# Two numbers that order the gathers and the heads of a PEER layer: OWN 64 to 0, HEADS regrouped

## The chip, the core and the metric

The kernel runs on one core of a Trainium2 chip. The metric is the device time of one execution in microseconds; lower is better. Each execution computes the whole model below, once. Engines are named as in the profile: PE is TensorE, DVE is VectorE, ACT is ScalarE, POOL is GpSimd, SP is SyncE (here it only starts DMAs).

## The reference

The input is 256 tokens of width 1024 in float32. Two blocks follow each other. The first has two layers, each a mixer (neighbourhood attention in layer 0, a short convolution in layer 1) and then a PEER feed-forward; the second block is attention, retention and projections. The change lies in PEER, which is computed twice, once per layer:

```python
q = (xc @ w_query).reshape(c, 8, 2, 128)              # 8 heads, 2 halves
sc = einsum('chpd,hpnd->chpn', q, keys)               # against 128 sub-keys each
sv, si = top_k(sc, 16)                                # 16 best of each half
cand = sv[:, :, 0, :, None] + sv[:, :, 1, None, :]    # 16 x 16 sums
best, pos = top_k(cand, 16); eidx = cidx at pos       # 16 experts per head of 16384
g = softmax(best)
a = einsum('cd,chkd->chk', xc, w_up[eidx])            # one dot product per chosen expert
out = einsum('chk,chkd->cd', gelu(a) * g, w_down[eidx])
```

Each token so has 8 x 16 = 128 chosen experts, called its numbers; w_up and w_down have 16384 rows of 1024 values per layer.

## The kernel before, in words

`peer(l)` treats the 256 tokens in three sets.

- Tokens 0 to 159 (`TU = 160`) are computed densely: all 16384 experts are run through PE in 128 blocks of 128 experts (`up(i)`, line 704), gelu is applied, and the result is multiplied by a mask that holds the gates of the chosen experts and zero elsewhere.
- Tokens 160 to 191 (the set `also`, 32 tokens) have their 128 dot products formed from gathered rows of w_up; the results enter the same mask, and from there the dense path.
- Tokens 192 to 255 (the set `own`, 64 tokens) have both the rows of w_up and the rows of w_down gathered, and never touch the dense path before the end.

One gather is an indirect DMA that POOL starts (line 592): 128 rows of 1024 float32 values, one row per partition. For `own`, 64 tokens by 2 halves of their numbers fill the partitions, so it needs 64 gathers for the dot products and 64 for the rows of w_down; `also` has 32 tokens by 4 quarters and needs 32 gathers. That makes 160 in each layer. Four buffers hold them (`GB`), and a gather is started at most three ahead of its use (`LOOK`). A use is one DVE instruction: a multiply with a sum for a dot product (line 606), a multiply-add into an accumulator for a row of w_down (line 616; line 614 for the first). After the last dot product of a set, ACT applies gelu (line 608), DVE multiplies by the gate (line 609), and for `also` transposes the result into `gT` (line 611).

PEER has these stages. In the stage of the heads, q and the scores are formed head by head in the order `HEADS`, and the top-k steps run behind them on DVE and POOL. After every second head `numbers(n)` (line 661) copies those expert numbers that are complete on all partitions of a set into its index tile. In the up stage, 128 blocks of w_up come from memory in 64 loads of 1 MB, and for each PE does eight matmuls per block; beside them, `build()` makes the mask, four tokens at a time (48 builds for 192 tokens: ACT lines 732 and 733, DVE line 736, PE line 738, then DVE line 744 or ACT line 746 into the piece `A`). In the down stage, 128 blocks of w_down come in 64 loads of 1 MB (line 846); each is split into two parts by ACT (line 219, `whi`) and DVE (line 220, `wlo`), and PE does ten matmuls of 512 columns per block (lines 819 to 829). Its left sides come from `A`, split by ACT and POOL (lines 756 and 757 for tokens 0 to 127, 842 and 843 for the rest).

The order of the work is set by the Python program, and a list scheduler then moves instructions where their inputs allow it. In the up stage one gathered row is used per 1/0.97 blocks (`USES`). In the down stage the uses that are left are spread evenly over the first 122 blocks, each placed behind the `wlo` of its block. The list of gathers and the places at which it matters are these:

```python
order = dots(own)[:OWN] + [x for s in also for x in dots(s)]    # 579
n_dots = len(order)
order += dots(own)[OWN:] + [(own, "down", m) for m in range(own.n)]
...
def build():
    t = built
    while t >= TU and head < n_dots:      # tokens 160 and up: first use up n_dots gathers
        use()
...
n0 = head                                 # at the end of the up stage
while head < len(order) and n0 + (len(order) - n0) * i // (NK - 6) >= head:   # block i, down stage
    use()
```

Of the kernel before, what the change touches and what calls it, by code (L numbers as in the profile page):

```python
# [36 lines left out]
GB = 4  # L37
UB = 3
LOOK = 3
HEADS = (0, 4, 1, 5, 2, 6, 3, 7)  # L40
STEPS = 8
SCB = 6
USES = 0.97
OWN = 64
BEND = 4
TDELAY = 9
EARLY = (0, 0, 4, 4, 4, 4, 6, 6)
# [38 lines left out]
class Kern:  # L86
# [434 lines left out]
    def peer(self, l):  # L521
        nc, tc, a, h = self.nc, self.tc, self.a, self.h
        with ExitStack() as ctx:
# [54 lines left out]
            dots = lambda s: [(s, "dot", m) for m in range(s.n)]  # L578
            order = dots(own)[:OWN] + [x for s in also for x in dots(s)]
            n_dots = len(order)  # L580
            order += dots(own)[OWN:] + [(own, "down", m) for m in range(own.n)]
            tiles, chosen = {}, []
# [70 lines left out]
            def numbers(n):  # L653

                done = HEADS[: n + 1]
                for s in sets:
# [8 lines left out]
            old = []  # L665
            for n, hh in enumerate(HEADS):
                marks.append(len(steps))
# [94 lines left out]
            for n in range(PH):  # L762
                heads(HEADS[n])
                if n > 0:
# [911 lines left out]
```

## Time and profile before

| | us |
|---|---|
| Median of 3 runs (2219.02 to 2224.34) | 2223.98 |
| The profiled execution, its own time | 2221.52 |
| Its span, from the first to the last instruction | 2219.8 |
| PE busy in the span | 2074.6 (93%) |
| DVE busy in the span | 1615.1 (73%) |

The span of 2219.8 us has 1.7 us around it that the trace doesn't show. In the 40 slices of the page one slice is 55.5 us. PE is at 9 (90% or more) in most of them. The up stage of layer 0 runs from about 290 to 530 us and its down stage from about 586 to 884 us; in layer 1 these are about 1160 to 1401 and 1454 to 1749 us. Between the up and the down stage of each layer the PE clock row has a dip, and so has PE's busy row.

### The profile page before, as it was taken

The page shows a single profiled execution, that of the slowest core. Times are in us where ns is not written, and L with a number is a line of the kernel's source. Part 1 is how long each engine was busy: PE and PEld are TensorE (multiplying, and loading weights), DVE is VectorE, ACT ScalarE, POOL GpSimd, SP SyncE. Part 2 cuts the span into 40 slices and gives each one's busy share as a digit, 9 for nine tenths or more (in the row PEclk, how much of TensorE's full clock was granted, in tenths as well). Part 3 has the DMA queues.
Part 4 walks back from the last instruction along what each step waited for, and adds up shares of the span by engine and source line. Part 5 has one row for each costly group of instructions (what it writes and reads, how often), then busy time and mean ns, then how long its engine had stood idle before and what let it go on. Part 6 is the DMA issues. An engine that isn't in the chain of part 4 may idle for free.

```text
span 2219.8 us, 34905 instructions
## 1 busy us (share of the span) xinstructions
PE 2074.6 (93%) x12576; PEld 1808.1 (81%) x12576; DVE 1615.1 (73%) x3458; ACT 1039.7 (47%) x2245; POOL 919.2 (41%) x780
## 2 busy tenths in 40 slices
PE   7999989995799999998898999499999999999998
PEld 6989989995677777998898999477777797568886
DVE  5869857786888887867865786778888766456674
ACT  4643225541555554544323553355555555445453
POOL 2437843334656663225863333575656111001100
PEclk9999999998799999999999999799999999699999
DMA  8576599999788886666579999888888664035543
GB/s 288 192 226 208 189 399 364 355 368 328 264 320 321 319 323 224 213 229 201 198 262 392 358 363 376 279 311 317 324 327 310 196 178 143 10 109 162 165 151 121
DMA packets 178733, 576.21 MB, mean 260 GB/s; under 512 B 16112, under 2 KB 77440, under 8 KB 145408
## 3 DMA queue, kind: packets, MB, share of 16 engines
q1 hardware_dynamic: 123840, 391.82, 50.6%
q0 software_dynamic: 48896, 172.25, 21.2%
q10 hardware_dynamic: 5824, 9.92, 1.5%
q8 instruction: 99, 1.62, 0.3%
q14 instruction: 74, 0.61, 0.1%
HBM read 568.49 MB, written 3.15 MB: 258 GB/s over the span
## 4 chain that ended last, share of the span: by engine, by line
PE 66%; issue 8%; DVE 7%; POOL 5%; DMA 3%; ACT 1%; POOLq 0%; DVEq 0%; ACTq 0%
PE acc L704 11%; PE acc L225 6%; PE acc L226 6%; PE acc L227 6%; PE acc L819 5%; PE acc L824 5%; PE acc L822 5%; PE acc L829 5%; PE acc L823 5%; POOL gt L592 3%; PE tp L738 3%; DMA gt<-in_peer_w_up_dram,one 2%; PE tp L1250 1%; DVE gt L606 1%; PE tp L1263 1%
## 5 line engine op out<-in xcount | busy, mean ns | idle before, releaser
L704 PE MATMUL acc<-one,up 128*128 128x160 f32 x4096 | 579.8, 301 | 13.7 <-DMA up<-in_up_T_dram 13.5
L704 PEld LDWEIGHTS acc<-one,up 128*128 128x128 f32 x4096 | 565.3, 192 | 15.1 <-issue 6.9
L220 DVE TENSOR_TENSOR wlo<-dn,whi 128x1024 fp32r<-128x1024 f32 x256 | 362.9, 1426 | 115.3 <-ACT whi L219 115.1
L219 ACT CAST whi<-dn 128x1024 fp32r<-128x1024 f32 x256 | 267.8, 1048 | 229.6 <-PE acc L824 178.1
L220 DVE TENSOR_TENSOR wlo<-raw,whi 128x1024 fp32r<-128x1024 f32 (+1 forms) x196 | 256.9, 1314 | 139.2 <-ACT whi L219 137.8
L592 POOL DMA_INDIRECT gt<-in_peer_w_up_dram,one x192 | 206.8, 1077 | 340.1 <-DVE gt L606 298.1
L606 DVE SCALAR_TENSOR_TENSOR gt<-gt,rows 128x1024 f32<-128x1024 f32 x192 | 239.5, 1258 | 100.4 <-DMA gt<-in_peer_w_up_dram,one 100.1
L219 ACT CAST whi<-raw 128x1024 fp32r<-128x1024 f32 (+1 forms) x212 | 219.9, 1038 | 197.9 <-PE acc L227 81.3
L592 POOL DMA_INDIRECT gt<-in_peer_w_down_dram,one x128 | 201.5, 1574 | 175.2 <-DVE rows L616 148.7
L819 PE MATMUL acc<-whi,ahl 128*128 128x512 f32 x512 | 201.9, 394 | 6.5 <-POOL ahl L843 6.5
L824 PE MATMUL acc<-whi,m 128*128 128x512 f32 x512 | 204.9, 400 | 2.2 <-POOL m L757 2.2
L829 PE MATMUL acc<-wlo,ahl 128*64 128x512 f32 x512 | 200.5, 392 | 0.0
L823 PE MATMUL acc<-wlo,o 128*128 128x512 f32 x512 | 200.2, 391 | 0.0
L738 PE MATMUL tp<-m,o 128*128 128x128 f32 x768 | 111.3, 297 | 67.4 <-DVE m L736 53.7
L616 DVE SCALAR_TENSOR_TENSOR rows<-gt,one,rows 128x1024 f32<-128x1024 f32 x126 | 163.6, 1298 | 7.1 <-DMA gt<-in_peer_w_down_dram,one 6.8
L822 PE MATMUL acc<-whi,o 128*128 128x512 f32 x512 | 163.5, 399 | 1.4 <-ACT o L756 1.4
L738 PEld LDWEIGHTS tp<-m,o 128*128 128x128 f32 x768 | 103.6, 210 | 72.1 <-DVE m L736 53.1
L715 ACT ACTIVATE one<-acc 128x320 f32<-128x320 f32 (+14 forms) x112 | 41.0, 367 | 226.9 <-PE acc L704 226.8
L819 PEld LDWEIGHTS acc<-whi,ahl 128*128 128x128 f32 x512 | 96.6, 189 | 58.9 <-POOL ahl L843 7.7
L225 PE MATMUL acc<-xhi,whi 128*128 128x256 f32 x448 | 129.0, 290 | 0.8 <-ACT xhi L170 0.8
L732 ACT ACTIVATE o<-one,one 128x128 f32<-128x128 f32 x384 | 122.7, 401 | 11.6 <-PE tp L738 11.3
L226 PE MATMUL acc<-xlo,whi 128*128 128x256 f32 x448 | 128.0, 287 | 0.0
(350 smaller groups left out, 4168.8 us busy)
## 6 DMA issues: line engine op xcount, KB each, us to landing
up<-in_up_T_dram SPq DMA_DIRECT2D x128, 1024.0 KB, 7.7
dn<-in_down_P_dram SPq DMA_DIRECT2D x128, 1024.0 KB, 6.4
raw<-in_l_w_in_dram SPq DMA_DIRECT2D x84, 512.0 KB, 3.7
raw<-in_peer_w_query_dram SPq DMA_DIRECT2D x32, 512.0 KB, 4.8
raw<-in_l_w_out_dram SPq DMA_DIRECT2D x28, 512.0 KB, 3.5
raw<-in_attn_w_qkv_dram SPq DMA_DIRECT2D x24, 512.0 KB, 5.1
raw<-in_conv_w_in_dram SPq DMA_DIRECT2D x24, 512.0 KB, 4.5
raw<-in_attn_w_o_dram SPq DMA_DIRECT2D x8, 512.0 KB, 3.8
```

Of the source, the lines that this page charges most:

```text
L219: self.last_hi = nc.scalar.copy(hi[:, :n], raw[:, :n])
L220: self.last_lo = (eng or nc.vector).tensor_tensor(lo[:, :n], raw[:, :n], hi[:, :n].bitcast(F32), op=OP.subtract)
L225: nc.tensor.matmul(out, lhi, rhi, start=start, stop=False)
L592: nc.gpsimd.indirect_dma_start(out=t, out_offset=None, in_=rows[kind], in_offset=bass.IndirectOffsetOnAxis(ap=s.idx[:, m : m + 1], axis=0) ...
L606: nc.vector.scalar_tensor_tensor(t, t, 1.0, s.x, op0=OP.mult, op1=OP.mult, accum_out=s.dot[:, m : m + 1])
L704: nc.tensor.matmul(ps[:, j * TU : (j + 1) * TU], raw[:, j, c], x32[:, c], start=c == 0, stop=c == 7)
L738: nc.tensor.matmul(ps[:, j * P : (j + 1) * P], o2[:, j], m1[:, j], start=True, stop=True)
L819: both = lambda: nc.tensor.matmul(acc[1][q], hl[:, k], whi, start=i == 0, stop=i == NK - 1)
L822: nc.tensor.matmul(acc[0][q], hi[:, k], whi, **st)
L823: nc.tensor.matmul(acc[0][q], hi[:, k], wlo, start=False, stop=False)
L824: nc.tensor.matmul(acc[0][q], lo[:, k], whi, start=False, stop=i == NK - 1)
L829: nc.tensor.matmul(acc[1][q][:HALF], hl[:, k, :HALF], wlo, start=False, stop=False)
```

## The change

Two constants are changed, and nothing else.

```diff
-HEADS = (0, 4, 1, 5, 2, 6, 3, 7)
+HEADS = (0, 4, 2, 6, 1, 5, 3, 7)
-OWN = 64
+OWN = 0
```

With `OWN = 64` the list was: 64 dot products of `own`, 32 of `also`, 64 rows of w_down; `n_dots` was 96. With `OWN = 0` it is: 32 of `also`, 64 of `own`, 64 rows of w_down; `n_dots` is 32. The new `HEADS` completes the first 16 numbers of `also` after four heads (its quarters hold heads 0 and 1, 2 and 3, 4 and 5, 6 and 7). For `own` (halves: heads 0 to 3 and 4 to 7) 16, 16, 48 and 64 numbers are complete after two, four, six and eight heads, where it was 16, 32, 48 and 64. `numbers` issues 14 small copies per layer in place of 16.

What this does to the order is seen in three places of layer 0. In the names below, `rows192` is the activations of `own` or its accumulator, `rows160` those of `also`, `us` is an up block after gelu, `m1` and `o2` are a build's masks (or later the split of `A`).

On DVE, before, the end of the up stage:

```order
L606 SCALAR_TENSOR_TENSOR gt_930_5208,one272_272_1448<-gt_930_5208,rows160_269_1445 128x1024
L719 TENSOR_TENSOR one642_642_3378<-one642_642_3378,us_925_5192 128x2x160
L606 SCALAR_TENSOR_TENSOR gt_931_5211,one272_272_1448<-gt_931_5211,rows160_269_1445 128x1024
L606 SCALAR_TENSOR_TENSOR gt_932_5214,one272_272_1448<-gt_932_5214,rows160_269_1445 128x1024
L719 TENSOR_TENSOR one642_642_3378<-one642_642_3378,us_964_5334 128x2x160
L606 SCALAR_TENSOR_TENSOR gt_933_5217,one272_272_1448<-gt_933_5217,rows160_269_1445 128x1024
L719 TENSOR_TENSOR one642_642_3378<-one642_642_3378,us_975_5402 128x2x160
...
L606 SCALAR_TENSOR_TENSOR gt_953_5277,one272_272_1448<-gt_953_5277,rows160_269_1445 128x1024
L614 TENSOR_SCALAR rows192_962_5322<-gt_954_5280,one268_268_1444 128x1024
L609 TENSOR_TENSOR one273_273_1449<-one273_273_1449,one271_271_1447 128x32
L611 STREAM_TRANSPOSE one262_262_1438<-one273_273_1449 128x32
L736 TENSOR_SCALAR m1_959_5293<-one4_4_80,one260_260_1436,one262_262_1438 128x128 x4
```

The same place on DVE in the changed kernel:

```order
L606 SCALAR_TENSOR_TENSOR gt_940_5277,one267_267_1443<-gt_940_5277,rows192_264_1440 128x1024
L736 TENSOR_SCALAR m1_951_5329<-one4_4_80,one260_260_1436,one262_262_1438 128x128 x4
L606 SCALAR_TENSOR_TENSOR gt_945_5311,one267_267_1443<-gt_945_5311,rows192_264_1440 128x1024
L736 TENSOR_SCALAR m1_956_5363<-one4_4_80,one260_260_1436,one262_262_1438 128x128 x4
L719 TENSOR_TENSOR one642_642_3376<-one642_642_3376,us_925_5191 128x2x160
...
L719 TENSOR_TENSOR one642_642_3376<-one642_642_3376,us_986_5551 128x2x160
L220 TENSOR_TENSOR wlo_995_5575<-dn_993_5572,whi_994_5574 128x1024
L606 SCALAR_TENSOR_TENSOR gt_980_5523,one267_267_1443<-gt_980_5523,rows192_264_1440 128x1024
L220 TENSOR_TENSOR wlo_998_5592<-dn_993_5572,whi_997_5591 128x1024
L220 TENSOR_TENSOR wlo_1001_5608<-dn_999_5605,whi_1000_5607 128x1024
```

Before, the dot products of `also`, then 609 and 611, stand ahead of the masks of the last eight builds (first `m1_959`). Now those masks stand among the up blocks, and the first `wlo` of the down stage comes right behind the last `us`.

On PE, before, at the change from the up to the down stage:

```order
L704 MATMUL acc_1005_5574<-one263_263_1439,up_1004_5572 128x160 x16
L704 MATMUL acc_1013_5622<-one263_263_1439,up_1012_5620 128x160 x16
L738 MATMUL tp_957_5291<-m1_959_5293,o2_958_5292 128x128 x4
...
L738 MATMUL tp_1007_5586<-m1_1009_5588,o2_1008_5587 128x128 x4
L822 MATMUL acc_1019_5660<-whi_1025_5669,o2_1015_5634 128x512
```

The same place on PE in the changed kernel:

```order
L738 MATMUL tp_968_5443<-m1_970_5445,o2_969_5444 128x128 x4
L704 MATMUL acc_958_5383<-one263_263_1439,up_957_5381 128x160 x16
L738 MATMUL tp_976_5491<-m1_978_5493,o2_977_5492 128x128 x4
L704 MATMUL acc_966_5431<-one263_263_1439,up_965_5429 128x160 x16
L704 MATMUL acc_974_5479<-one263_263_1439,up_973_5477 128x160 x16
L704 MATMUL acc_982_5527<-one263_263_1439,up_981_5525 128x160 x16
L822 MATMUL acc_988_5565<-whi_994_5574,o2_984_5539 128x512
```

Eight groups of line 738 (one per build) stood behind the last up block; now they stand before it, and the first down matmul follows the last up matmul.

On DVE in the down stage, before, around the 40th block:

```order
L220 TENSOR_TENSOR wlo_1172_6388<-dn_1170_6385,whi_1171_6387 128x1024
L616 SCALAR_TENSOR_TENSOR rows192_962_5322<-gt_1144_6259,one268_268_1444,rows192_962_5322 128x1024
L220 TENSOR_TENSOR wlo_1175_6405<-dn_1170_6385,whi_1174_6404 128x1024
L220 TENSOR_TENSOR wlo_1178_6421<-dn_1176_6418,whi_1177_6420 128x1024
L616 SCALAR_TENSOR_TENSOR rows192_962_5322<-gt_1152_6306,one268_268_1444,rows192_962_5322 128x1024
L220 TENSOR_TENSOR wlo_1181_6438<-dn_1176_6418,whi_1180_6437 128x1024
```

And in the changed kernel, around the same block:

```order
L616 SCALAR_TENSOR_TENSOR rows192_1092_6054<-gt_1128_6224,one268_268_1444,rows192_1092_6054 128x1024
L220 TENSOR_TENSOR wlo_1152_6326<-dn_1150_6323,whi_1151_6325 128x1024
L616 SCALAR_TENSOR_TENSOR rows192_1092_6054<-gt_1137_6264,one268_268_1444,rows192_1092_6054 128x1024
L220 TENSOR_TENSOR wlo_1155_6343<-dn_1150_6323,whi_1154_6342 128x1024
L220 TENSOR_TENSOR wlo_1158_6359<-dn_1156_6356,whi_1157_6358 128x1024
L616 SCALAR_TENSOR_TENSOR rows192_1092_6054<-gt_1140_6281,one268_268_1444,rows192_1092_6054 128x1024
```

The down stage holds more uses per block than before. The program reaches its end of the up stage with 110 gathers used before and 80 now (before, the loop in `build()` ran 30 uses in one go just before block 114; now it finds `also` done some 35 blocks earlier), so 50 and 80 are left for the down stage of each layer.

## Rows read from the trace of the kernel before

**Rows 1.** Windows by stage: us, busy of PE, PEld, DVE, ACT, POOL, PEclk, DMA share, GB/s.

```profile
290.00:330.00 40.00, 33.10 (x232) 32.50 (x233) 22.51 (x53) 13.81 (x43) 12.30 (x12) 0.91 1.02 412
...
340.00:490.00 150.00, 150.00 (x1156) 150.00 (x1156) 118.23 (x369) 85.72 (x301) 50.71 (x48) 1.00 0.97 361
...
490.00:529.60 39.60, 38.99 (x283) 38.26 (x282) 22.58 (x43) 5.04 (x14) 15.05 (x14) 1.00 0.93 359
529.60:586.00 56.40, 17.88 (x75) 14.93 (x74) 45.70 (x77) 21.43 (x71) 35.36 (x29) 0.63 0.81 266
586.00:592.40 6.40, 6.40 (x16) 4.54 (x17) 3.39 (x3) 1.24 (x2) 5.28 (x4) 0.54 0.45 140
600.00:860.00 260.00, 260.00 (x1129) 199.62 (x1128) 213.09 (x159) 141.70 (x169) 154.87 (x101) 1.00 0.87 318
...
1401.30:1453.60 52.30, 18.48 (x74) 15.26 (x74) 41.85 (x73) 21.36 (x71) 33.89 (x27) 0.61 0.80 265
1470.00:1720.00 250.00, 250.00 (x1086) 191.89 (x1085) 204.85 (x153) 136.62 (x165) 150.25 (x98) 1.00 0.88 321
```

**Rows 2.** PE in order of time, layer 0: start, us, instructions, idle before and releaser.

```profile
411.31 1.50 PE L738 MATMUL tp<-m,o 128*128 128x128 f32 x12
412.65 4.51 PE L704 MATMUL acc<-one,up 128*128 128x160 f32 x32
...
520.71 8.93 PE L704 MATMUL acc<-one,up 128*128 128x160 f32 x64 [0.17 <-DMA up<-in_up_T_dram]
555.85 2.07 PE L738 MATMUL tp<-m,o 128*128 128x128 f32 x8 [26.20 <-DVE m L736]
...
585.96 0.79 PE L819 MATMUL acc<-whi,ahl 128*128 128x512 f32 x1 [4.36 <-POOL ahl L843]
```

**Rows 3.** The same in layer 1.

```profile
1383.63 17.63 PE L704 MATMUL acc<-one,up 128*128 128x160 f32 x128 [1.06 <-DMA up<-in_up_T_dram]
...
1453.57 0.51 PE L819 MATMUL acc<-whi,ahl 128*128 128x512 f32 x1 [2.17 <-POOL ahl L843]
```

**Rows 4.** DVE in order of time, layer 0, behind the dot products.

```profile
555.20 0.21 DVE L611 STREAM_TRANSPOSE one<-one 128x32 f32<-128x32 f32 x1
555.45 1.11 DVE L736 TENSOR_SCALAR m<-one,one,one 128x128 f32<-128x128 f32 x4
```

**Rows 5.** ACT in order of time, layer 0, around the last up block.

```profile
529.68 0.44 ACT L718 ACTIVATE us<-acc 128x320 f32<-128x320 f32 x1 [3.91 <-PE acc L704]
530.05 2.94 ACT L219 CAST whi<-dn 128x1024 fp32r<-128x1024 f32 x3
...
578.56 0.74 ACT L842 CAST ahl<-one 128x256 fp32r<-128x256 f32 x2
```

**Rows 6.** Lines 220, 616 (DVE), 757, 843 (POOL), 600 to 860 us: ns min/median/max.

```profile
L220 DVE TENSOR_TENSOR wlo<-dn,whi x113: 1207/1226/2927, 599.5 to 858.8; 128x1024 fp32r<-128x1024 f32 x113
  ACT whi L219: 47.3, 67
...
L616 DVE SCALAR_TENSOR_TENSOR rows<-gt,one,rows x46: 1270/1275/1280, 603.0 to 857.6; 128x1024 f32<-128x1024 f32 x46
...
L757 POOL TENSOR_TENSOR m<-one,o x29: 1282/1310/2282, 597.9 to 855.3; 128x512 fp32r<-128x512 f32 x29
...
L843 POOL TENSOR_TENSOR ahl<-one,ahl x28: 743/756/1725, 606.2 to 854.6; 128x256 fp32r<-128x256 f32 x28
```

**Rows 7.** Line 220 alone, same stretch: us, busy of DVE and POOL, PEclk, DMA, GB/s.

```profile
600.00:860.00 260.00, 160.74 (x113) 0.00 (x0) 1.00 0.87 318
```

**Rows 8.** DMA issues of 600 to 860 us: KB each, median us to landing.

```profile
dn<-in_down_P_dram SPq DMA_DIRECT2D x56, 1024.0 KB, 6.0
gt<-in_peer_w_down_dram,one POOLq DMA_INDIRECT x44, 7.2
```

**Rows 9.** The same for 340 to 490 us.

```profile
up<-in_up_T_dram SPq DMA_DIRECT2D x28, 1024.0 KB, 7.7
```

**Rows 10.** Line 606, 0 to 1000 us: what ended DVE's idle time (us, times).

```profile
  DMA gt<-in_peer_w_up_dram,one: 48.4, 25
```

## The prediction

> **What bounds the kernel now.** I read the windows by stage first, then PE in order of time where they show a hole, then the engines around it. In the steady up stage PE is busy 150.00 of 150 us and in the down stage 260.00 of 260 [rows 1]. A saving of work on DVE, POOL or DMA is worth nothing there. Between the two stages it is otherwise: from 529.6 to 586.0 us PE is busy 17.88 of 56.40 us, in layer 1 18.48 of 52.30, at a granted clock of 0.63 and 0.61 [rows 1]. The last up matmul of layer 0 ends at 520.71 + 8.93 = 529.64; then PE waits 26.20 us for line 736 on DVE, and the regular run of the down stage begins at 585.96 [rows 2]. Layer 1: 1383.63 + 17.63 = 1401.26 and 1453.57 [rows 3]. The mask of line 736 starts at 555.45, right behind the transpose of `also` at 555.20 [rows 4]. That is the forced loop in `build()`: tokens 160 and up want `gT`, and the list puts the 32 dot products of `also` behind all 64 of `own`, so the program uses 30 gathers in one go at block 114, and eight builds queue behind them. By the windows DMA is at 0.81 and DVE at 45.70 of 56.40 us [rows 1], so this is a chain of single gathers, masks and copies with PE idle.
>
> **What the change removes: the hole.** I count what PE does in it at full clock.
> - Eight builds are 64 records of line 738. Twelve take 412.65 - 411.31 = 1.34 us [rows 2], so 0.112 each and 7.1 us for 64.
> - A down matmul takes 260.00 / 1129 = 0.230 us [rows 1].
> - Layer 0, from 529.64 until the clock is back at about 592.4: 62.8 us, with 7.1 us of builds and 75 + 16 - 64 = 27 other records, some of the up stage's end; I take 24, 5.5 us. Lost: 62.8 - 7.1 - 5.5 = 50.2.
> - Layer 1: 52.3 us, at full clock from 1453.57 on, with 7.1 and 74 - 64 = 10 records, 2.3: lost 42.9.
> - Together 93 us.
>
> With the new list `also` is done after 32 uses, some 35 blocks before its first build, so its chain (lines 608, 609, 611) hides under up blocks. The eight builds go between the last up blocks, where PE pays their 7.1 us, already counted as work. What is late next is the start of the down stage. The last up block frees the buffer that the first `whi` needs, so behind its matmul ACT does 718 (0.44), 842 (0.74 for two, so 0.37) and 219 (2.94 for three, so 0.98) [rows 5]: 1.8 us, then 1.2 for `wlo` [rows 6]; PE has four matmuls (0.9) meanwhile. The second `wlo` stands behind a use, another 0.5 to 1.5. I take 4 us a layer with a dip of the clock, 8 in all; the bounds are 2 (the bare 1.8) and 12 (as long as the 6.4 us at clock 0.54 [rows 1], twice).
>
> **What it moves: 30 uses per layer into the down stage.** 110 gathers were used before that stage and now 80, so its first 122 blocks take 80 uses in place of 50: 0.656 per block instead of 0.41. A block is ten matmuls, 2.30 us of PE. Three things have to fit under it.
> - DVE is busy 213.09 of 260 us [rows 1]; 260 / 2.30 = 113 blocks, 1.89 us per block. A use is 1.275 us [rows 6] and overlaps its neighbour by some 0.07, so 0.246 x 1.2 = 0.30 more: 2.19 of 2.30, 95% in place of 82%. It fits, with 0.11 us to spare.
> - Contention with POOL takes from that. `wlo` has a median of 1.226 us and a maximum of 2.93 [rows 6]; its 113 sum to 160.74 [rows 7], 22.2 us more than 113 times the median. That is 0.39 us for each of the 57 instructions of lines 757 and 843 in the stretch, whose shortest take 1.28 and 0.74 [rows 6]. They now often fall into DVE's idle time (47.3 us of waits for `whi` [rows 6]), which the uses fill up.
> - DMA: a block loads 0.524 MB and gathers 0.656 x 0.524, 0.868 MB in 2.30 us, 377 GB/s, up from 318. The up stage carried 361 with PE full, and 412 was moved where PE waited [rows 1]. A load landed in 6.0 us in the down stage and 7.7 in the up stage [rows 8, 9]. By the buffers the load of a pair has about 8 us between the `wlo` that frees it and the cast that wants it, so slack is small.
>
> The nearest ends: 0 if all three stay under PE, and on the other side DVE blocked fully for each POOL instruction. Two lines, 1.28 + 0.74 us per four blocks, are 0.51 per block, of which 0.20 is paid: 1.89 + 0.30 + 0.31 = 2.50, 0.18 to 0.20 per block, 46 to 51 us over 256 blocks. DMA held to the up stage's 361 GB/s would be 0.868 / 0.361 = 2.40, 26 us. I take 0.07 per block, 18 us: half of the new POOL overlap plus scatter eats the 0.11 that is free and a little more.
>
> The Trainium skill, page "SBUF — State Buffer", section "Who interferes with whom", has the rule that speaks against this change: a DVE instruction with two SBUF inputs and a GpSimd instruction that reads SBUF exclude each other, and whoever comes second blocks until the first is done. The `wlo` rows, with a maximum of a whole instruction above the median, agree. By that rule the full end (46) becomes the sum where DVE has no idle time left, which is the second rival below; with the measured 0.39 carried over unchanged it would be 0.
>
> **What costs nothing.** The new `HEADS` reorders loads of equal size. The first 16 numbers of `also` are complete after four heads, the rest after eight; the first uses come behind the softmax in either kernel, so the gathers wait for nothing new; two fewer copies of `numbers` save POOL time that PE doesn't wait for. I allow 3 us either way. Gelu and gate of `own` now fall into the down stage, once per layer, DVE waiting for ACT: 1 to 2 us if DVE is full, inside the 18.
>
> **Sum.** 2221.5 (the profiled execution) - 93 + 8 + 18 = 2154.5. The median of the runs stands 2.5 above that execution, so 2157.
>
> **Rivals.**
> - Everything fits under PE: down blocks stay at 2.30 us. For it: none of DVE, ACT, POOL, DMA reaches its limit by the sums; against it: two of them are within 5%. 2139.
> - DVE becomes the bound of the down stage through the POOL contention: 46 in place of 18, 2185. For it: 95% before any new contention; against it: part of the POOL work still finds DVE waiting.
> - Slower than before: DVE waits for gathers. A use stands in DVE's queue ahead of the next `wlo`, so a late gather holds back PE. It decides from a loss of 85 us, 0.33 per block, (0.33 + 0.11) / 0.656 = 0.7 us of wait at each use; at 1.0 us it is (0.66 - 0.11) x 256 = 140 us, 2279. For it: 25 waits of 48.4 us in all for the dot products of layer 0 [rows 10]; against it: those are in stretches where uses are run as fast as the gathers land. The new pace, 2.30 / 0.656 = 3.5 us per use, is slower than the up stage's (a block's 0.524 x 1.97 MB at 361 GB/s are 2.9 us, a use per 2.9), where PE was full, and a gather is started three uses ahead, 10.5 us against 7.2 to landing [rows 8].
> - The change doesn't do what it says, since something else makes PE wait between the stages as long: within a few us of 2224. The order of the instructions speaks against it: the first down matmul stands behind the last up matmul.
>
> **How the numbers follow.** The forecast (2146 to 2170) has 0.58, DVE bound 0.19, everything under PE 0.14, slower 0.05, no effect 0.04. The range 2133 to 2190 takes in the second and the third. A measurement of this kernel can tell about 0.3% (7 us) from no change. Faster 0.91, same 0.04, slower 0.05.
>
> **What will show it.** Between the last matmul of line 704 and the first of 822 PE waits 2 to 5 us, not 26, and no line 738 stands in between; the clock stays near 1.0. Line 611 ends long before the first build of tokens 160 and up. In the down stage DVE is 92 to 98% busy, DMA 0.95 to 1.0 at 365 to 377 GB/s, PE 96 to 99%; where PE waits it is for `wlo`. It is wrong if PE waits there for gathers through line 616 or 606, if the loads of line 846 land late so that ACT waits for DMA, or if a block takes over 2.5 us.

## The result and the profile after

The changed kernel takes 2143.28 us (median of 4 runs, 2140.8 to 2145.78) against 2223.25 before (median of 4); the ratio is 0.9644 (95% interval 0.9625 to 0.9663). The forecast was 2157, its range 2133 to 2190. The profiled execution has a span of 2139.7 us, 80.1 less than the one before.

First the windows by stage of the changed kernel (columns as in [rows 1]); the stretches answer to the up stage, its end, the start of the down stage, and the down stage.

```profile
340.00:490.00 150.00, 150.00 (x1156) 150.00 (x1155) 118.94 (x372) 85.01 (x297) 49.39 (x47) 1.00 0.97 360
490.00:540.00 50.00, 49.99 (x381) 49.74 (x380) 27.90 (x71) 24.48 (x86) 15.38 (x14) 1.00 0.81 304
539.99:544.00 4.01, 2.17 (x8) 1.48 (x9) 2.76 (x3) 3.88 (x6) 0.77 (x2) 1.00 0.00 0
560.00:820.00 260.00, 256.68 (x1105) 194.30 (x1104) 255.06 (x195) 139.63 (x168) 219.32 (x128) 1.00 0.97 370
...
1400.00:1650.00 250.00, 245.96 (x1058) 185.94 (x1057) 242.50 (x183) 132.06 (x159) 206.87 (x121) 1.00 0.97 368
```

The hole of [rows 1] (56.4 and 52.3 us with PE busy a third of the time) is gone, and the clock stays at 1.00. In the down stage DVE is busy 98% (82% before), POOL 84% (60%), DMA 0.97 (0.87), and PE still 98.7% and 98.4%.

PE in order of time at the turn of layer 0, to be held against [rows 2], and of layer 1, against [rows 3]:

```profile
525.89 1.05 PE L738 MATMUL tp<-m,o 128*128 128x128 f32 x8
526.78 13.21 PE L704 MATMUL acc<-one,up 128*128 128x160 f32 x96
541.75 0.50 PE L822 MATMUL acc<-whi,o 128*128 128x512 f32 x1 [1.76 <-ACT whi L219]
...
543.01 0.51 PE L823 MATMUL acc<-wlo,o 128*128 128x512 f32 x1
```

```profile
1354.78 11.03 PE L704 MATMUL acc<-one,up 128*128 128x160 f32 x80
1367.57 0.50 PE L822 MATMUL acc<-whi,o 128*128 128x512 f32 x1 [1.76 <-ACT whi L219]
...
1371.67 0.44 PE L829 MATMUL acc<-wlo,ahl 128*64 128x512 f32 x1 [0.72 <-DVE wlo L220]
```

The last build stands before the last up blocks. PE waits 1.76 us for the first `whi`, then 0.7 for the second `wlo`, where it waited 26.2 and 24.0 us for the masks.

The transposes of `also`, one per layer (min/median/max ns, first and last start); before, the one of layer 0 started at 555.20, after the last up block [rows 4]:

```profile
L611 DVE STREAM_TRANSPOSE one<-one x2: 204/208/211, 377.0 to 1200.4; 128x32 f32<-128x32 f32 x2
```

In the down stage, the waits of ACT and of DVE between 560 and 820 us (total us, times, longest us):

```profile
ACT whi L219 <- PE acc L824: 59.5, 62, 1.4
ACT whi L219 <- DMA dn<-in_down_P_dram: 31.9, 16, 3.5
...
DVE wlo L220 <- ACT whi L219: 3.4, 8, 1.0
DVE rows L616 <- DMA gt<-in_peer_w_down_dram,one: 1.3, 2, 0.9
```

DVE waited 47.3 us for `whi` before [rows 6], now 3.4: it has become a queue that is nearly always full. ACT now waits 31.9 us for loads, for which its list had no wait before in this layer; they land after 7.7 us (6.0 in [rows 8]). PE itself waits for `wlo` alone, and SP, which starts the loads, waits for the `wlo` that frees a buffer (same stretch):

```profile
PE acc L829 <- DVE wlo L220: 3.1, 4, 1.4
...
SPq L846 <- DVE wlo L220: 235.5, 54, 7.0
```

So the late `wlo` is what PE sees. Whether it is late because DVE is full or because its load came late, these lists don't say; run e7 below does.

The same stretch by line on DVE and POOL (ns min/median/max), against [rows 6]:

```profile
L220 DVE TENSOR_TENSOR wlo<-dn,whi x110: 1206/1213/2997, 561.0 to 818.8; 128x1024 fp32r<-128x1024 f32 x110
...
L616 DVE SCALAR_TENSOR_TENSOR rows<-gt,one,rows x61: 1268/1276/2327, 604.5 to 820.0; 128x1024 f32<-128x1024 f32 x61
...
L757 POOL TENSOR_TENSOR m<-one,o x28: 1281/2279/2298, 563.8 to 815.6; 128x512 fp32r<-128x512 f32 x28
...
L843 POOL TENSOR_TENSOR ahl<-one,ahl x28: 743/1074/2111, 563.1 to 814.9; 128x256 fp32r<-128x256 f32 x28
```

On DVE the minima and medians stand; the maximum of line 616 goes from 1.28 to 2.33 us, so that the uses now collide with POOL too. On POOL the median of line 757 goes from 1.31 to 2.28 us: it now nearly always meets a busy DVE.

To set the runs side by side I use, in each trace, the time from the first transpose of line 643 (the up stage proper begins) to the first matmul of line 862 (the down stage has ended): "up and down". It was 884.3 - 289.4 = 594.9 and 1749.0 - 1156.4 = 592.6 us before, and is 846.1 - 292.9 = 553.2 and 1672.9 - 1118.4 = 554.5 after: 41.7 + 38.1 = 79.8 of the 80.1 us. Two more traces of the changed kernel (e0 and e10 below) differ from this one by up to 5.2 us per layer, so single traces are no finer than that.

### The profile page after: what moved, and what is told of

It reads as the page before. It is cut to its first block, busy times and chain, and to the rows that moved or that the text cites. A ratio compares the mean times of both kernels' runs of the same rounds, so it can differ in the third digit from the quotient of the medians.

```text
span 2139.7 us, 34866 instructions
## 1 busy us (share of the span) xinstructions
PE 2057.4 (96%) x12576; PEld 1788.6 (84%) x12576; DVE 1639.8 (77%) x3458; ACT 1040.3 (49%) x2245; POOL 977.0 (46%) x776
## 4 chain that ended last, share of the span: by engine, by line
PE 61%; DVE 18%; DMA 10%; issue 5%; POOL 3%; ACT 2%; ACTq 0%; SPq 0%; DVEq 0%; POOLq 0%
PE acc L704 20%; PE acc L225 7%; PE acc L226 7%; PE acc L227 7%; DVE wlo L220 6%; PE tp L738 4%; DMA dn<-in_down_P_dram 3%; DVE rows L616 3%; DMA gt<-in_peer_w_down_dram,one 2%; DMA up<-in_up_T_dram 2%; PE acc L829 2%; PE acc L819 2%; PE acc L824 2%; PE acc L823 2%; PE acc L822 2%
## 5 line engine op out<-in xcount | busy, mean ns | idle before, releaser
L592 POOL DMA_INDIRECT gt<-in_peer_w_up_dram,one x192 | 220.0, 1146 | 329.0 <-DVE gt L606 280.5
L592 POOL DMA_INDIRECT gt<-in_peer_w_down_dram,one x128 | 222.5, 1738 | 47.8 <-DVE rows L616 21.7
L616 DVE SCALAR_TENSOR_TENSOR rows<-gt,one,rows 128x1024 f32<-128x1024 f32 x126 | 188.3, 1494 | 3.7 <-DMA gt<-in_peer_w_down_dram,one 3.5
L757 POOL TENSOR_TENSOR m<-one,o 128x512 fp32r<-128x512 f32 x64 | 133.6, 2087 | 5.0 <-ACT o L756 5.0
L227 PE MATMUL acc<-xhi,wlo 128*128 128x256 f32 x448 | 126.3, 284 | 0.0
```

The lines of the kernel that those rows point to most:

```text
L227: return nc.tensor.matmul(out, llo, rhi, start=False, stop=stop)
L592: nc.gpsimd.indirect_dma_start(out=t, out_offset=None, in_=rows[kind], in_offset=bass.IndirectOffsetOnAxis(ap=s.idx[:, m : m + 1], axis=0) ...
L616: nc.vector.scalar_tensor_tensor(accD, t, s.act[:, m : m + 1], accD, op0=OP.mult, op1=OP.add)
```

## The experiments

| run | median us | ratio to before (95%) | up and down, layers 0 and 1 |
|---|---|---|---|
| changed kernel | 2143.3 | 0.9644 (0.9625 to 0.9663) | 553.2, 554.5 |
| e1_old_heads | 2147.6 | 0.9688 (0.9662 to 0.9713) | 557.7, 553.0 |
| e2_heads_alone | 2220.3 | 0.9996 (0.9971 to 1.0022) | 594.6, 592.4 |
| e3_own32 | 2145.7 | 0.9688 (0.9661 to 0.9714) | 554.8, 557.8 |
| e4_own48 | 2165.7 | 0.9765 (0.9739 to 0.9792) | 567.2, 568.2 |
| e0_changed_again | 2142.7 | 0.9637 (0.9616 to 0.9657) | 558.4, 555.3 |
| e5_uses080 | 2188.5 | 0.9850 (0.9824 to 0.9875) | 587.0, 576.2 |
| e6_uses115 | 2159.7 | 0.9715 (0.9692 to 0.9737) | 567.2, 561.2 |
| e7_narrow_use | 2131.3 | 0.9592 (0.9565 to 0.9619) | 547.4, 551.1 |
| e8_tail_uses | 2136.0 | 0.9619 (0.9595 to 0.9644) | 550.3, 553.8 |
| e9_tail_old_heads | 2139.9 | 0.9634 (0.9610 to 0.9657) | 550.2, 546.1 |
| e10_changed_third | 2145.3 | 0.9644 (0.9615 to 0.9674) | 555.9, 556.0 |

Three groups were measured together, each with its own runs of before: e1 to e4, then e0 and e5 to e7, then e8 to e10. The medians of before were 2219.2, 2222.1 and 2222.1 us.

**Which of the two numbers does it.** Against the changed kernel:

```diff
-HEADS = (0, 4, 2, 6, 1, 5, 3, 7)     # e1
+HEADS = (0, 4, 1, 5, 2, 6, 3, 7)
-OWN = 0                              # e2
+OWN = 64
```

> OWN = 0 with the old order of heads. Theory (the gain is the forced run of 30 uses that is gone, and HEADS does nothing to the time): 2143 us, within 7. Rival (the new order of heads is needed, since the numbers of the 32-token set are complete later without it and its gathers wait): some 10 to 40 us slower than the changed kernel, with DVE or POOL waiting for gathers at the start of the up stage.

> The new order of heads with OWN = 64. Theory: 2223 us, within 7, with the hole of 50 us between the stages of each layer as before. Rival (the order of heads brings part of the gain): below 2210.

OWN does it. With the new heads alone nothing changes, and the wait for the mask is there (PE, layer 0):

```profile
560.19 2.08 PE L738 MATMUL tp<-m,o 128*128 128x128 f32 x8 [26.23 <-DVE m L736]
```

With the old heads and OWN = 0 nearly the whole gain is there, 4 us short of the changed kernel by medians that were not measured together. That remainder was tried again with e0 and e9.

**Is it the forced run, or how early `also` is done?**

```diff
-OWN = 0
+OWN = 32     # e3: also at places 32 to 63 of the list, nothing forced
+OWN = 48     # e4: also at places 48 to 79, 14 uses forced
```

> OWN = 32: 32 dot products of the 64-token set, then the 32-token set, then the rest; n_dots is 64, and at the first build of tokens 160 and up the program has made 65 uses, so nothing is forced. Theory (only the forced run matters, not how early the 32 tokens are done): 2143 to 2150 us. Rival (it matters how early the 32-token set is done, since gelu, gate and transpose stand close ahead of the builds): 2165 to 2185, with PE waiting for line 736 before the eight last builds.

> OWN = 48: 14 uses are forced at block 114 in place of 30. Theory: the forced run takes about 14 x 1.9 = 27 us of DVE, which the last 14 up blocks (2.2 us each, 31 us) just hide, but the eight builds (2.7 us of ACT each) come behind it, so some 15 to 20 us per layer stay lost: 2165 to 2185 us. Rival (the hole is proportional to the forced uses, 14 of 30): 23 us per layer, 2180 to 2195. Rival (any forced run stops PE as long as before): 2215 or more.

e3 is within 3 us of the changed kernel by its median, and its ratio is that of e1, measured with it, though its transpose starts at 479.5 us in layer 0, 102.5 us later than in the changed kernel:

```profile
L611 DVE STREAM_TRANSPOSE one<-one x1: 204/204/204, 479.5 to 479.5; 128x32 f32<-128x32 f32 x1
```

So it doesn't matter, as far as these runs resolve, how early the set is done, only that no uses are forced ahead of its builds. e4 gives a dose in between. PE, around the end of its up stage:

```profile
526.28 0.71 PE L738 MATMUL tp<-m,o 128*128 128x128 f32 x4 [3.42 <-DVE m L736]
...
544.67 1.95 PE L738 MATMUL tp<-m,o 128*128 128x128 f32 x16
552.40 3.78 PE L738 MATMUL tp<-m,o 128*128 128x128 f32 x16 [5.79 <-ACT o L733]
559.12 0.79 PE L824 MATMUL acc<-whi,m 128*128 128x512 f32 x1 [2.05 <-POOL m L757]
```

14 of 30 forced uses cost 14.0 and 13.7 us per layer in this trace, about a third of the 41.7 and 38.1 of the full run. The traced execution is the slowest of e4's four; by medians e4 stands 18 to 20 us behind e1 and e3, 9 to 10 per layer. The forced uses hide under the last up blocks but for a wait of 3.42 us for line 736; what shows besides is builds that come behind the last up block (32 records, four of the eight in layer 0) and a wait of 5.79 us among them, behind which 16 records of line 738 take 3.78 us in place of 1.95 (granted clock 0.50 from 552 to 565 us, the lower of TensorE's two levels, 1.2 GHz). The time lies at the low end of the theory's range, below the proportional rival's.

**What does the down stage still lose, and to whom?**

```diff
-USES = 0.97
+USES = 0.8                                                          # e5: 94 uses left for the down stage
+USES = 1.15, and `if owed >= 1.0` becomes `while owed >= 1.0`       # e6: 65 left
-nc.vector.scalar_tensor_tensor(accD, t, s.act[:, m : m + 1], accD, ...)
+nc.vector.scalar_tensor_tensor(accD[:, :64], t[:, :64], s.act[:, m : m + 1], accD[:, :64], ...)    # e7
```

> The changed kernel itself, as the yardstick on the chip on which the next three run: 2143 us, within 7. With it the rerun of the old order of heads (2147.6) can be judged: theory (HEADS does nothing) says that this run's ratio to before is the same 0.968 to 0.969; the rival (HEADS is worth some 4 us) 0.966 or lower.

> USES = 0.8 in place of 0.97, with OWN = 0: 94 uses are left for the down stage in place of 80, 0.77 per block. Theory (the down stage stands at the edge: DVE needs 2.26 of the 2.30 us of a block now, and each further use per block costs 1.2 us plus its part of the contention): 0.115 x 1.2 + 0.05 = 0.19 more, 2.45 per block, some 15 us per layer lost, 2165 to 2185 us, DVE at 99%. Rival (DVE still has room, or the loads decide and take it): 2143 to 2150.

> USES = 1.15, and the uses owed are all made at once, with OWN = 0: 65 uses are left for the down stage. Theory (the up stage is at its limit too, by DMA: 0.524 x 2.15 = 1.13 MB per block, 3.0 us at 373 GB/s against 2.74 of PE): up to 20 us per layer lost in the up stage and 4 won in the down stage, 2150 to 2175 us. Rival (DMA still has room to the 412 GB/s seen, so the gathers are free there): 2135 to 2140.

> The changed kernel, but the multiply-add of a gathered row of w_down (line 616) covers 64 of 1024 columns; the gathers are unchanged, so DMA and POOL do all they did, and DVE is relieved of some 1.15 us per use. Left out: the other 960 columns of that sum. Theory (what the down stage still loses, 3.3 us in 260 and 4.0 in 250, is DVE's queue): PE waits under 1 us in such a stretch, 2133 to 2138 us, and waits of ACT for the loads stay. Rival (the loads of w_down landing late are the loss): PE waits as before, 2143 us.

e7 takes work from DVE; the gathers and the loads stay (windows, 560 to 820 us, and what DVE and ACT wait for):

```profile
560.00:820.00 260.00, 260.00 (x1129) 199.45 (x1128) 195.08 (x199) 141.92 (x170) 162.31 (x128) 1.00 0.98 375
...
DVE wlo L220 <- ACT whi L219: 62.0, 55, 2.4
...
ACT whi L219 <- DMA dn<-in_down_P_dram: 10.2, 5, 2.6
```

PE is busy 260.00 of 260 us with DMA at 375 GB/s, more than in the changed kernel. So the loads aren't the loss; a full DVE frees their buffers later, and with that relieved the waits of ACT for them fall from 31.9 to 10.2 us, where the theory had them stay. The traces of the changed kernel agree: in e0 ACT waits 51.7 us for loads in this stretch and PE only 2.5 for `wlo`. From the last up matmul to line 862 e7 takes 300.6 and 301.8 us against 306.1 and 307.1 (e0: 306.3 and 306.2, e10: 309.3 and 306.9): DVE costs the changed kernel 10.8 us in both layers together. By medians e7 is 11.3 us faster than e0. POOL is relieved too (219.32 to 162.31 us), as DVE holds up its instructions less (line 757 is back at a median of 1.31 us); but in the changed kernel no wait of PE in this stretch is for POOL.

e5 goes the other way (windows, and DVE's waits):

```profile
560.00:820.00 260.00, 241.37 (x1002) 177.61 (x1001) 242.63 (x206) 125.85 (x152) 207.03 (x126) 0.98 0.95 356
...
DVE rows L616 <- DMA gt<-in_peer_w_down_dram,one: 9.7, 12, 2.5
```

1002 records are 100 blocks, 2.59 us each; DVE is busy 2.42 of them, 93% and not the 99% of the theory, and all of PE's waits are for `wlo`. The theory had 2.45 for DVE and expected that to be the block; it left out that a DVE without slack also waits for gathers in its own order, 9.7 us here and 2.6 for the last dot products. e5 is 45.8 us behind the changed kernel's rerun by medians, where the theory had 22 to 42. (The traced execution is the slowest of its six, 16 us above the median, so the sizes in it are upper ends.) This is the mechanism of the "slower" rival, clear at 94 uses and small at 80 (1.3 us).

e6's time lies in the theory's range, but by luck: the reason is another. From line 643 to the last up matmul it takes 252.0 and 247.5 us (247.1 and 247.4 in the changed kernel, 252.1 and 249.2 in e0), so DMA wasn't the limit of the up stage; but the scheduler put no more than 88 of the 95 uses ahead of the first `wlo`, and the others came in a heap into the first ten down blocks:

```profile
556.67 1.23 DVE L606 SCALAR_TENSOR_TENSOR gt<-gt,rows 128x1024 f32<-128x1024 f32 x1 [3.52 <-DMA gt<-in_peer_w_up_dram,one]
...
560.10 1.75 DVE L606 SCALAR_TENSOR_TENSOR gt<-gt,rows 128x1024 f32<-128x1024 f32 x1
561.78 2.30 DVE L606 SCALAR_TENSOR_TENSOR gt<-gt,rows 128x1024 f32<-128x1024 f32 x1
```

A second gap follows near 610 us: PE waits 4.3 us for a `wlo`, and there ACT waits 5.1 us for a load and DVE 2.7 and 2.5 us for gathers, with DMA at 411 to 425 GB/s from 606 to 612 us. So late transfers stand behind PE's wait here. How much of e6's 17 us each of the two gaps makes isn't shown.

**A better place for six uses.** Before the turn, DVE is busy 2.04 and POOL 3.25 of 15.7 us in the changed kernel, and DMA is at 0.40:

```profile
526.00:541.70 15.70, 13.99 (x105) 13.74 (x103) 2.04 (x4) 4.28 (x12) 3.25 (x4) 1.00 0.40 145
```

```diff
-owed += USES if len(A) == 4 and own.ready else 0.0                          # e8; e9 with the old HEADS too
-if owed >= 1.0 and head < issued:
+owed += (USES if i < 122 else 2.0) if len(A) == 4 and own.ready else 0.0
+while owed >= 1.0 and head < issued:
```

> The changed kernel, but in the last six up blocks two uses per block are made in place of 0.97: six uses more before the first wlo, 74 left for the down stage in place of 80. In the changed kernel DVE, POOL and DMA stand nearly still from 527 to 541 us of layer 0. Theory (the down stage loses only what DVE's queue costs, at most 5 us per layer as the narrow uses showed, and six of 80 uses are 0.06 us per block of DVE): 1 to 3 us faster than the changed kernel on the same chip. Rival (the uses delay the last gelu products or the first wlo, as the larger number of uses did at USES = 1.15): 5 to 15 us slower.

> The same with the old order of heads. Theory (HEADS does nothing to the time): within 4 us of the run before it on the same chip. Rival (the new order is worth some 4 us, as the earlier pair of 2147.6 and 2143.3, taken on two chips, would have it): 4 to 8 us slower than it.

> The changed kernel as the yardstick of these two: 2143 us, within 7.

e8 has the lowest median of the kernels that leave nothing out, 9 us under the changed kernel measured with it (the theory had 1 to 3), and its down stage agrees (259.32 us of PE in 260):

```profile
560.00:820.00 260.00, 259.32 (x1121) 197.71 (x1120) 245.60 (x187) 140.74 (x170) 204.89 (x121) 1.00 0.96 361
```

But the intervals 0.9595 to 0.9644 and 0.9615 to 0.9674 overlap, so the times alone don't show a gain over the changed kernel. The traces point to one: from the last up matmul to line 862 e8 takes 302.9 and 303.6 us and e9 304.1 and 301.2, where three traces of the changed kernel take 306.1 to 309.3.

For HEADS the evidence is mixed. e0's expectation came out on the rival's side: its ratio is 0.9637, below 0.966, and its interval doesn't touch that of e1 (0.9662 to 0.9713), though the two were not measured together. e9 against e8 is again 4 us by medians, with overlapping intervals. Against it, e2 has no effect at `OWN = 64`, e3 with the new heads has the ratio of e1 with the old, and in the up and down stages e9 is not slower than e8 (550.2 and 546.1 against 550.3 and 553.8). An effect of the new heads of some 4 us (0.2%) can't be excluded; the runs don't settle it.

## Why the prediction was right, step by step

- **The number.** The forecast was 13.7 us too slow, and the band that it gave itself (2146 to 2170) just misses 2143.3; the time lies in the wider range. Between the sum, 2154.5, and the traced execution, 2141.4, are 13.1 us: 8.0 from the start of the down stage and the stage itself (below), and 4.8 from the up stages, which grew by 9.4 us where the moved builds were put at 14.2. The second is no finding: in e0's trace they grew by 16.1.
- **The hole, 93 us lost.** Right in place, and in size to some 2 us. From the last up matmul to line 862 took 354.7 and 347.7 us before and takes 306.1 and 307.1 now, 89.2 less. By the prediction's count, 14.2 of that are the builds, which moved ahead of the last up matmul as said. With the hole gone entirely it would be 93 + 14.2 = 107.2; so 18.0 us came back, where the forecast had 8 + 18 = 26. The two losses that were measured by themselves make 4.9 + 10.8 = 15.7 of the 18.0; the other 2.3 have no cause shown. e2 and e4 show the hole whole and in part.
- **The start of the down stage, 8 us.** Too dear: the wait is 1.76 + 0.7 us per layer, 4.9 in all, its first part as the sum of ACT's rows said, but the clock didn't fall for it; the granted clock is 1.00 in that stretch. The allowance for a dip was not needed.
- **The down stage, 18 us.** The mechanism was right (PE waits there for `wlo` alone), the size was off: 10.8 by e7. Contention between `wlo`, the uses and POOL was put at half of what is left, 0.155 us per block; it is (159.00 - 110 x 1.213 + 90.07 - 61 x 1.276) / 110 = 0.34 against 22.2 / 113 = 0.20 before, so about 0.15 more (159.00 and 90.07 us are the sums of lines 220 and 616 in that stretch). What I added for scatter was too much: DVE could run at 98% with PE losing 1.3%.
- **HEADS costs nothing.** Right within the 3 us that it allowed for e2 (0.9996 of before); with `OWN = 0` some 4 us in favour of the new heads stay open.
- **The rivals.** By its number "everything fits" at 2139 was nearer (4 us) than the forecast, but it is not what happens: PE waits for `wlo`, and e7 shows the 10.8 us. DVE as the bound is real at 80 uses already, at 10.8 us and not 46. Waits for gathers (slower) are small at 80 uses and clear at 94 (e5).
- **A sign of being wrong that came up.** The prediction named loads that land late so that ACT waits for them. ACT does wait, 31.9 us, and yet the account holds, since e7 shows that these waits aren't PE's loss. As a sign it was badly chosen.
- The rest nearly cancels. The code behind the down stage of layer 1, which is the same in both, took 470.8 us before and 466.8 after; the code ahead of the first up stage took 3.5 us longer after (292.9 against 289.4). In the traces of before, e2, e4, e5 and e6 the code behind takes 470.8 to 472.0 us, in the others 466.8 to 469.8; no run shows why.

## What to carry to other kernels

A loop that says "use up everything ahead of this" hides in a list's order: look at where a stage with a full engine ends, and which set of the work that its last steps need stands behind work that nobody needs yet. Before moving work into a stage that is full on one engine, count the next engine's time per step, contention included: here DVE at 98% cost PE 1.3%, 10.8 us in all, and 14 more uses in each layer cost 45.8 us on top (e5). Where an in-order engine has no slack left, lateness of the loads behind it can be a symptom; relieve that engine and leave the transfers as they are to see which it is.

## What the hardware showed that I had not expected

- A PE idle time of 1.76 us left the granted clock at 1.00 (539.99 to 544.00 us). The hole with its 26.2 us of waiting stood at a mean of 0.63, with 0.54 in the 6.4 us behind it [rows 1], and in e4 the clock was at 0.50 from 552 to 565 us, behind a wait of 5.79 us. 1.00 is 2.4 GHz, 0.50 is 1.2 GHz, and a mean between them mixes the two.
- When DVE and POOL collide, both pay, and how full DVE is shifts the shares. With DVE at 98%, 56 POOL instructions of lines 757 and 843 cost DVE 38 us, 0.68 each, and took 39 us more than at their shortest themselves (61.03 + 34.79 - 28 x (1.281 + 0.743), the sums and minima of the two lines). Before, with DVE at 82%, it was 22 us for DVE and 23 for POOL; in e7, at 75%, 29 for DVE (169.22 - 114 x 1.226) and 4 for POOL. In the changed kernel's stretch all 51 instructions of lines 220 and 616 that took over 0.1 us more than their shortest overlap one of lines 757 or 843; 101 of the others overlap a gather and are no longer for it (by the start and end times of the trace).
- The Trainium skill, "SBUF — State Buffer", section "Who interferes with whom", has an exclusive lock between a DVE instruction with two SBUF inputs and a GpSimd instruction that reads SBUF: whoever comes second blocks until the first is done. By that the loss of DVE would be some 1.0 us each, the mean of 1.28 and 0.74, if DVE always came second and right behind the start. The 0.68 agrees with blocking, and with DVE coming second, or that early, only in part of the cases.
- Single executions of this kernel spread more than first seen: before ran from 2211.1 to 2231.9 us in the 13 runs beside e1 to e4.
